# Layer 0's modulation vectors: four of six chunks moved out of the FFN's up-projection, two into the norms ahead of layer 0's mixer, two into its attention

## The chip, the cores and the metric

The kernel runs on one core of a Trainium2 chip. The metric is the device time of one execution in microseconds (us), lower is better. The kernel before takes 2705.91 us, the median of three runs (2704.4 to 2709.71).

## What is computed

One launch computes two blocks on 512 tokens of width 1024 in float32. The first block is a mixer of three kinds (a linear recurrence, forgetting attention, an RWKV cell) with a gated FFN. The second has two layers; each normalises, modulates by vectors that come from a condition, mixes (window attention with rope and a sink, neighbourhood attention, a gated convolution) and ends in a mixture of experts. The part that the change moves is `adaln`, for six chunks of 1024 columns per layer:

```python
def adaln(cond, w_mod_l, b_mod_l, n_chunks):
    m = jax.nn.silu(cond) @ w_mod_l[:, :n_chunks * D_MODEL] + b_mod_l[:n_chunks * D_MODEL]
    return jnp.split(m, n_chunks, axis=-1)
...
    for l in range(DEPTH_2):
        last = l == DEPTH_2 - 1
        sh1, sc1, g1, sh2, sc2, g2 = [m[:, None, :] for m in adaln(c, w_mod[l], b_mod[l], N_MOD)]
        ctx_mod = adaln(c_ctx, w_mod[l], b_mod[l], 2 if last else N_MOD)
        h = modulate(x, sh1, sc1)
        u = h @ w_in_l
        ...
        x = layer_norm(DEEPNORM_ALPHA * x + g1 * o, ln1_g[l], ln1_b[l])
        h2 = modulate(x, sh2, sc2)
        x = layer_norm(DEEPNORM_ALPHA * x + g2 * ec_moe(h2, w_router[l], w_gate[l], w_up[l], w_down[l]),
                       ln2_g[l], ln2_b[l])
```

So chunks 0 and 1 (sh1, sc1) are needed ahead of layer 0's mixer, chunks 2 to 5 only behind its attention.

## The kernel before, in words

The kernel is written in a tile framework: the program is written in one order, and the framework's scheduler sets a fixed order of instructions for each engine, with semaphores between them. Each engine then works through its own queue in order. The engines are TensorE (PE: products and transposes), VectorE (DVE), ScalarE (ACT, which also issues some DMAs), GpSimd (POOL) and SyncE (SP, which issues most DMAs, weight loads among them).

Precision comes from splitting: a weight tile `wr` is loaded, ScalarE rounds it to `wh` (L287), VectorE makes the rest `wl` (L288), and each product is three matmuls, hi by hi, lo by hi, hi by lo (L149, through `mm`).

`modulations(jobs, tile_, tag)` (L1013) makes one chunk of 1024 modulation columns for both conditions (token and context). For each of eight row blocks k it loads 128 x 1024 of w_mod, 512 KB, on SP's queue (L1021) into a tile that the caller's `tile_` gives, and issues four matmuls of 2 x 256, one to each column group of the array (L152, through `mmt`). It yields after every four k, so that the caller can place the steps. Then ScalarE copies the four pieces out of PSUM (L1028), eight small transposes turn them into columns (L1031), and VectorE adds the bias into the table of modulation columns (L1032). A chunk is thus 8 loads, 32 matmuls, 4 copies, 8 transposes and 1 add; in the trace a matmul of this kind is two records.

Stages around the change, in time:
- the FFN's up-projection of the first block, about 420 to 703 us: 44 blocks of 128 columns, each a weight load, a GEMM over 514 columns and a small convolution in ScalarE and VectorE. In its loop 12 modulation steps (6 chunks of layer 0) are spread;
- the FFN's down-projection with other modulation work, and the first block's last norms;
- `layer(0)`: layer norms (lnc), `modulated`, which normalises, transposes (xn, L1227) and splits tokens and context into `hh` and `hl`; then gated halves b = 0 and 1, each two GEMMs from `gemm2` (w_in loads L1259), a gate `sg` (a tanh) and the product `hx` (L1291, L1294); then 62 convolution taps on VectorE (`cy`, L1300 and L1303), placed by `tick` among the attention's work;
- attention: `stack_k` and `stack_q` make keys and queries by `gemm2`. With rope (`rope`, L1312) the queries are copied (L1315), their halves are swapped by eight DMAs on SP (L1318, L1319), multiplied on POOL and VectorE (L1320 to L1322) and split into `qst` (L1362, L1363). `scores`, `softmax` and `attend` follow for the head pairs i = 0 to 3 and four query blocks j. The sinks `nsk` (L1381, L1382) and tables `tb` (L1386) are loaded on ScalarE's queue. In the last head pair, i == 3, each query block also takes one modulation step of layer 1's chunks 0 and 1, with weight staging tiles (tags wr, wh, wl, two buffers each) as loads' targets (`any_w`).

In the changed kernel the lines from L1243 on have numbers higher by 3.

Of the kernel before, what the change touches and what calls it, by code (L numbers as in the profile page):

```python
# [9 lines left out]
F32 = mybir.dt.float32  # L10
# [129 lines left out]
def body(tc, A, out):  # L140
# [13 lines left out]
    offs, _, offs2, _ = host_constants()  # L154
# [17 lines left out]
    def nm(s):  # L172
        _n[0] += 1
        return "%s_%d" % (s, _n[0])
# [876 lines left out]
    def finish_modulations(after, after2):  # L1051
# [9 lines left out]
        for i in range(8):  # L1061
# [2 lines left out]
        DV.tensor_tensor(mc3, pt.rearrange("p (i g z) -> p g i z", i=8, g=4)[:, :, :, 0],  # L1064
                         v2[:, 80:112].rearrange("p (g i) -> p g i", g=4), ALU.add)
    sums_ = []
    mods = modulations([(0, six) for six in range(6)],
                       lambda: mrp.tile([128, 1024], F32, name=nm("wm"), tag="wm", bufs=8))
    for i in range(22):
        res = []  # L1070
        for hf in range(2):
            for _ in range(12 * (2 * i + hf + 1) // 44 - 12 * (2 * i + hf) // 44):
                next(mods, None)
            blk = 22 * hf + i
            W = load_w(wup, 5632, 128 * blk, 128)
            ps = gemm_fm(gps(), W, 0, 128, h2h, h2l, 0, 514)
            t = cv.tile([128, 512], F32, name=nm("cv"), tag="cv%d" % hf)
            AC.activation(t, ps[:, 2:514], AF.Copy, scale=fcol[:, 2, blk:blk + 1])  # L1078
            DV.scalar_tensor_tensor(t, ps[:, 1:513], fcol[:, 1, blk:blk + 1], t, ALU.mult, ALU.add)
            DV.scalar_tensor_tensor(t, ps[:, 0:512], fcol[:, 0, blk:blk + 1], t, ALU.mult, ALU.add)  # L1080
            res.append(t)
        AC.activation(res[0], res[0], AF.Gelu_apprx_tanh)
        DV.tensor_tensor(res[1], res[0], res[1], ALU.mult)
        AC.activation(aH[:, i, :], res[1], AF.Copy)
        DV.tensor_tensor(aL[:, i, :], res[1], f(aH[:, i, :]), ALU.subtract)
# [45 lines left out]
    mods = late_modulations()  # L1131
# [56 lines left out]
    def layer(l):  # L1188
        full = l == 0
# [47 lines left out]
        if full:  # L1237
            modulated(cxn, NC_, 512, 1)
            modulated(layer_norms(X, lnc), 512, 0, 0)
            cxs.close()  # L1240
        else:
            cb = [tp.tile([128, D], F32, name=nm("cb")) for j in range(2)]
            modulated(ready["x"], 512, 0, 0)  # L1243
            skewed([ready["ctx"](j, tp, cb[j]) for j in range(2)])
            modulated(cb, NC_, 512, 1)
            ready["close"]()
            cts.close()
# [232 lines left out]
        def any_w():  # L1480
            wtags.append(wtags.pop(0))
            return WPw.tile([128, 1024], F32, name=nm("wm"), tag=wtags[0], bufs=WB[0])
        mods = modulations([(1, 0), (1, 1)], any_w, "m") if full else iter(())

        def mod_steps(n):
            for _ in range(n):
# [21 lines left out]
        for i in range(4):  # L1508
# [4 lines left out]
            for j in range(4):  # L1513
                a0, a1 = max(0, j - 1), min(3, j + 1)
                w = 128 * (a1 - a0 + 1)
                ts = []
                for h in range(2):
                    ps = gps()
                    if j < 3:
                        c0, segs = 512 - w, [(512 - w, 128 * a0, w), (512, 512, 256)]  # L1520
                    else:
                        c0, segs = 256, [(256, 512, 256), (512, 128 * a0, w)]
                    scores(ps, q, k, h, 128 * j, segs)
                    b0 = (384, 256, 256, 0)[j]
                    ts.append(softmax([(ps[:, c0:c0 + w + 256], C2("wb")[:, b0:b0 + w + 256])], i + 4 * h))
                xb = list(range(a0, a1 + 1))
                attend(ts, xb + [4, 5] if j < 3 else [4, 5] + xb, (0, 64), oT[:, i, 128 * j:128 * j + 128])
                tick(NT)
                if i == 3:
                    mod_steps(1)  # L1530
            if full:
                ctx_pair(q, k, (i, i + 4), (0, 64), i, 1)
# [773 lines left out]
```

## Time and profile before

| | |
|---|---|
| runs, median (range) | 2705.91 us (2704.4 to 2709.71) |
| profiled execution, its own time | 2706.21 us |
| its span in the profile | 2704.4 us |
| mean granted TensorE clock | 0.964 of full |
| PE, DVE, ACT, POOL busy | 93%, 45%, 32%, 6% of the span |
| the FFN's up-projection | about 420 to 703 us |
| last norms and first GEMM of layer 0 | 841 to 873 us |
| attention of layer 0 | about 950 to 1140 us |

Busy PE means that a matmul is in its pipeline; matmuls overlap, so starts tell the pace better than durations. The chain of work that ended last is followed back from the last instruction; what does not lie on it costs nothing by itself.

### The profile page before, as it was taken

How to read it: one execution, taken by the hardware profiler on the slowest of the kernel's cores; microseconds unless marked ns; L12 is line 12 of the kernel's file. 1: busy time of each engine (PE TensorE's matmuls, PEld its weight loads, DVE VectorE, ACT ScalarE, POOL GpSimd, SP SyncE). 2: the span in 40 equal slices, each digit the busy share in tenths (PEclk: the TensorE clock that was granted, in tenths of full speed). 3: DMA queues.
4: the chain of work that ended last, by engine and by line, in shares of the span. 5: the costliest groups of instructions: out<-in, count | busy, mean ns of one | idle time of the engine just before them, and what ended most of it. 6: DMA issues, size and time to landing. Idle time of an engine off the chain costs nothing.

```text
span 2704.4 us, 52343 instructions
## 1 busy us (share of the span) xinstructions
PE 2507.4 (93%) x22270; PEld 1724.3 (64%) x22270; DVE 1210.7 (45%) x2278; ACT 875.9 (32%) x1585; POOL 167.4 (6%) x260
## 2 busy tenths in 40 slices
PE   7999999999998999996999999997999969999996
PEld 7877868999876977675555555544877744333332
DVE  4435655555655986556212121216977631112112
ACT  4335544343215266633100000006267421111102
POOL 0010100000001011002100000001111010000000
PEclk9989999999998999997999999998999969999998
DMA  4211144555672231433899999991331459999997
GB/s 138 63 41 37 45 164 156 180 164 180 201 257 75 74 73 33 134 106 140 311 407 375 381 367 382 364 379 45 100 78 35 162 193 404 406 409 409 409 409 278
DMA packets 266986, 579.02 MB, mean 214 GB/s; under 512 B 39920, under 2 KB 130416, under 8 KB 266496
## 3 DMA queue, kind: packets, MB, share of 16 engines
q1 hardware_dynamic: 255712, 550.82, 55.5%
q0 software_dynamic: 4928, 13.18, 2.0%
q10 hardware_dynamic: 6112, 11.68, 1.3%
q8 instruction: 175, 2.87, 0.4%
q14 instruction: 59, 0.48, 0.1%
HBM read 560.85 MB, written 5.24 MB: 209 GB/s over the span
## 4 chain that ended last, share of the span: by engine, by line
PE 52%; DVE 9%; ACT 3%; issue 2%; DMA 2%; POOL 1%; DVEq 0%; POOLq 0%; ACTq 0%; SPq 0%
PE g L149 18%; PE a L149 12%; PE g L152 12%; PE a L152 6%; DVE cy L1303 2%; PE a L1432 2%; POOL rv L235 1%; DMA gr<-rows,rowi 0%; DVE y L2055 0%; DMA wr<-in_w_out_dram 0%; DMA ew<-in_w_up_dram 0%; PE a L2266 0%; ACT pT L1393 0%; ACT ht L1229 0%; DVE wl L288 0%
## 5 line engine op out<-in xcount | busy, mean ns | idle before, releaser
L149 PE MATMUL g<-ew,xsel 128*64 128x512 f32 x1024 | 249.7, 599 | 0.2 <-DMA ew<-in_w_up_dram 0.2
L152 PE MATMUL g<-ew,xsel 128*32 128x256 f32 x4096 | 247.8, 380 | 0.2 <-ACT xsel L1816 0.2
L288 DVE TENSOR_TENSOR wl<-wr,wh 128x1024 fp32r<-128x1024 f32 x95 | 115.4, 1215 | 170.8 <-ACT wh L287 161.1
L152 PEld LDWEIGHTS g<-ew,xsel 128*32 128x32 f32 x4096 | 132.4, 110 | 92.7 <-issue 7.6
L149 PEld LDWEIGHTS g<-ew,xsel 128*64 128x64 f32 x1024 | 74.0, 137 | 136.2 <-issue 123.2
L287 ACT ACTIVATE wh<-wr 128x1024 fp32r<-128x1024 f32 x95 | 99.7, 1050 | 186.3 <-PE g L149 122.1
L235 POOL TENSOR_TENSOR rv<-ru,epsc 128x1 f32<-128x1 f32 (+3 forms) x63 | 53.6, 855 | 1712.4 <-DVE ru L233 1299.9
L149 PE MATMUL g<-h2h,wh 128*128 128x256 f32 x704 | 143.8, 285 | 0.0
L149 PE MATMUL g<-h2l,wh 128*128 128x256 f32 (+1 forms) x704 | 142.2, 284 | 0.0
L149 PE MATMUL g<-h2h,wl 128*128 128x256 f32 x704 | 141.9, 283 | 0.0
L152 PE MATMUL a<-ew,xsel 128*32 128x256 f32 x2048 | 133.7, 379 | 0.0
L2170 DVE TENSOR_TENSOR sg<-sg,g 128x512 f32<-128x512 f32 x16 | 11.0, 688 | 272.0 <-ACT sg L2169 272.0
L149 PE MATMUL g<-ew,hT 128*64 128x512 f32 x512 | 127.0, 596 | 6.2 <-DVE y L2055 5.9
L152 PE MATMUL g<-ew,hidT 128*32 128x512 f32 x1024 | 127.3, 592 | 0.5 <-DVE hidT L2171 0.5
L149 PEld LDWEIGHTS g<-h2h,wh 128*128 128x128 f32 x704 | 109.9, 191 | 5.5 <-ACT cv L1078 3.1
L2257 DVE TENSOR_TENSOR hid<-sg,g 128x512 f32<-128x512 f32 x16 | 11.0, 686 | 225.6 <-ACT sg L2256 225.6
L149 PEld LDWEIGHTS g<-h2h,wl 128*128 128x128 f32 x704 | 109.7, 191 | 0.0
L149 PEld LDWEIGHTS g<-h2l,wh 128*128 128x128 f32 x704 | 109.1, 190 | 0.0
L2169 ACT ACTIVATE sg<-g 128x512 f32<-128x512 f32 x16 | 9.6, 597 | 305.8 <-PE g L152 305.8
L1303 DVE SCALAR_TENSOR_TENSOR cy<-hx,cvc,cy 128x798 f32<-128x798 f32 (+1 forms) x120 | 107.0, 927 | 1.8
L1412 ACT ACTIVATE p<-p,mx 128x768 f32<-128x768 f32 (+4 forms) x120 | 91.5, 763 | 19.9 <-DVE mx L1405 15.8
L152 PEld LDWEIGHTS a<-ew,xsel 128*32 128x32 f32 x2048 | 67.0, 110 | 44.0
(655 smaller groups left out, 5368.9 us busy)
## 6 DMA issues: line engine op xcount, KB each, us to landing
ew<-in_w_gate_dram SPq DMA_DIRECT2D x256, 512.0 KB, 10.2
ew<-in_w_up_dram SPq DMA_DIRECT2D x256, 512.0 KB, 10.1
ew<-in_w_down_dram SPq DMA_DIRECT2D x256, 512.0 KB, 10.1
wm<-in_w_mod_dram SPq DMA_DIRECT2D x96, 512.0 KB, 4.9
wr<-in_ffn_up_dram SPq DMA_DIRECT2D x44, 512.0 KB, 4.1
wr<-in_w_in_dram SPq DMA_DIRECT2D x42, 512.0 KB, 4.1
wr<-in_ffn_down_dram SPq DMA_DIRECT2D x22, 512.0 KB, 4.7
wr<-in_w_out_dram SPq DMA_DIRECT2D x16, 512.0 KB, 3.5
```

Source lines behind the costliest of these rows:

```text
L149: return PE.matmul(o, l, r, start=start, stop=stop, skip_group_check=True)
L152: PE.matmul(o, l, r, start=start, stop=stop, skip_group_check=True, tile_position=(0, o.start_partition()))
L235: PL.tensor_tensor(v[:P], u[:P], epsc[:P, :w], ALU.pow)
L287: AC.activation(hi, raw, AF.Copy)
L288: DV.tensor_tensor(lo, raw, f(hi), ALU.subtract)
L1303: DV.scalar_tensor_tensor(cy[b], hx[b][:, i:i + N], cvw[l][:, 2 * i + b:2 * i + b + 1], cy[b], ALU.mult, ALU.add)
L1412: AC.activation(t[:, :e], t[:, :e], AF.Exp, scale=-1.0, bias=m, accum_out=sm)
L1432: PE.transpose(ps[:, 128 * i:128 * i + 128], t[:, 128 * i:128 * i + 128], ident)
L2169: AC.activation(sg[:, :w], ps[:, 0:w], AF.Silu)
L2170: DV.tensor_tensor(sg[:, :w], sg[:, :w], ps[:, w:2 * w], ALU.mult)
L2257: DV.tensor_tensor(hid[:, 512 * n:512 * n + 512], sg, psx[:, 512:1024], ALU.mult)
```

## The change

The FFN's loop keeps chunks 0 and 1 of layer 0 (4 steps). Chunks 2 and 4 are made in `layer(0)` right behind the second `modulated`, with their own pool `mw` of eight 512 KB tiles. Chunks 3 and 5 are put ahead of layer 1's chunks in the attention's list, whose steps are now taken in head pairs 2 and 3.

```diff
@@ -1064,12 +1064,12 @@
     sums_ = []
-    mods = modulations([(0, six) for six in range(6)],
+    mods = modulations([(0, six) for six in range(2)],
                        lambda: mrp.tile([128, 1024], F32, name=nm("wm"), tag="wm", bufs=8))
     for i in range(22):
         res = []
         for hf in range(2):
-            for _ in range(12 * (2 * i + hf + 1) // 44 - 12 * (2 * i + hf) // 44):
+            for _ in range(4 * (2 * i + hf + 1) // 44 - 4 * (2 * i + hf) // 44):
                 next(mods, None)
@@ -1237,6 +1237,9 @@
             modulated(layer_norms(X, lnc), 512, 0, 0)
+            mw = e3.enter_context(tc.tile_pool(name="mw", bufs=1))
+            for _ in modulations([(0, 2), (0, 4)], lambda: mw.tile([128, 1024], F32, name=nm("wm"), tag="wm", bufs=8)):
+                pass
             cxs.close()
@@ -1480,7 +1483,7 @@
-        mods = modulations([(1, 0), (1, 1)], any_w, "m") if full else iter(())
+        mods = modulations([(0, 3), (0, 5), (1, 0), (1, 1)], any_w, "m") if full else iter(())
@@ -1526,7 +1529,7 @@
                 tick(NT)
-                if i == 3:
+                if i > 1:
                     mod_steps(1)
```

The scheduler makes of it another order on several engines. Three places are shown; the numbers behind names count buffers and differ between the two programs, and a row with x4 stands for four instructions.

TensorE, in the first GEMM of layer 0's gated half (g, from hh and hl), behind the last transposes of xn. Before:

```order
L149 MATMUL g_9095<-hl_8951,wh_9099 128x256
L1227 MATMUL a_9079<-con,xn_9008 128x128
L1227 MATMUL a_9079<-con,xn_9010 128x128
L1227 MATMUL a_9079<-con,xn_9012 128x128
L1227 MATMUL a_9079<-con,xn_9014 128x128
L149 MATMUL g_9095<-hh_8950,wl_9100 128x256
L149 MATMUL g_9095<-hh_8950,wh_9099 128x256
```

Now:

```order
L149 MATMUL g_8971<-hl_8695,wh_8975 128x256
L152 MATMUL a_8835<-wm_8836,scol 2x256 x4
L152 MATMUL a_8835<-wm_8842,scol 2x256 x4
L152 MATMUL a_8835<-wm_8848,scol 2x256 x4
L152 MATMUL a_8835<-wm_8854,scol 2x256 x4
L152 MATMUL a_8835<-wm_8860,scol 2x256 x4
L152 MATMUL a_8835<-wm_8866,scol 2x256 x4
L152 MATMUL a_8835<-wm_8872,scol 2x256 x4
L152 MATMUL a_8835<-wm_8878,scol 2x256 x4
L149 MATMUL g_8971<-hh_8694,wl_8976 128x256
L149 MATMUL g_8971<-hh_8694,wh_8975 128x256
```

Chunk 2's matmuls (wm, scol) stand as one block behind two more GEMM rows that follow those transposes. Chunk 4's eight groups stand further on, each alone behind five GEMM rows, and the small transposes in pairs, the last pair eight GEMM rows ahead of its end.

VectorE, where hx is made. Before, the sinks' row (nsk, L1382) stands ahead of the gate and the products, and a weight split between hx and the first tap:

```order
L1382 TENSOR_SCALAR nsk_9523<-nsk_9523 128x8
L288 TENSOR_TENSOR wl_9219<-wr_9216,wh_9218 128x1024
L1287 TENSOR_SCALAR sg_9205<-sg_9205 128x768
L1291 TENSOR_TENSOR hx_9208<-g_9096,sg_9205 128x512
L1294 TENSOR_TENSOR hx_9208<-g_9096,sg_9205 128x256
L288 TENSOR_TENSOR wl_9273<-wr_9270,wh_9272 128x1024
L1300 TENSOR_SCALAR cy_8939<-hx_9208,cvc_4906 128x798
```

Now:

```order
L1032 TENSOR_TENSOR mc_4904<-a_8953,v_4912 128x16
L1290 TENSOR_SCALAR sg_9081<-sg_9081 128x768
L1294 TENSOR_TENSOR hx_9084<-g_8972,sg_9081 128x512
L1297 TENSOR_TENSOR hx_9084<-g_8972,sg_9081 128x256
L1385 TENSOR_SCALAR nsk_9399<-nsk_9399 128x8
L1303 TENSOR_SCALAR cy_8683<-hx_9084,cvc_4906 128x798
```

The sinks' row now stands between hx and the first tap; on ScalarE the load that it waits for now stands behind the gate's tanh.

TensorE, ahead of the first scores of the last head pair (g, from kh and qst). Before, its rows are attends (pT, vx) of the head pair ahead and modulation groups; the last GEMM row of the queries stands some 50 rows further up:

```order
L1432 MATMUL a_11736<-con,p_11722 128x128 x2
L149 MATMUL a_11741<-pT_11734,vx_9337 64x128
L152 MATMUL a_11902<-wm_11921,scol 2x256 x3
L149 MATMUL a_11741<-pT_11739,vx_9337 64x128
L149 MATMUL a_11741<-pT_11734,vx_9338 64x128
L149 MATMUL a_11741<-pT_11739,vx_9338 64x128
L152 MATMUL a_11902<-wm_11988,scol 2x256 x4
L152 MATMUL a_11902<-wm_11994,scol 2x256 x4
L149 MATMUL g_11848<-kh_10550,qst_11805 128x256
L149 MATMUL g_11848<-kl_10551,qst_11805 128x256
```

Now:

```order
L149 MATMUL a_11737<-hh_8694,wl_11743 128x512
L149 MATMUL a_11738<-hh_8694,wl_11743 128x256
L1031 MATMUL a_11896<-con,wm_11891 128x2 x8
L152 MATMUL a_11906<-wm_11907,scol 2x256 x4
L152 MATMUL a_11906<-wm_11913,scol 2x256 x4
L152 MATMUL a_11906<-wm_11919,scol 2x256 x4
L152 MATMUL a_11906<-wm_11925,scol 2x256 x4
L152 MATMUL a_11906<-wm_11992,scol 2x256
L149 MATMUL g_11837<-kh_10426,qst_11794 128x256
L149 MATMUL g_11837<-kl_10427,qst_11794 128x256
```

The queries' GEMM (a, from hh, wh and wl) ends right ahead of eight transposes, four groups and one more matmul, and the scores follow.

## Rows read from the trace of the kernel before

**Rows 1.** The page: engines' busy time; DMA rate in 40 slices; the chain by engine

```profile
PE 2507.4 (93%) x22270; PEld 1724.3 (64%) x22270; DVE 1210.7 (45%) x2278; ACT 875.9 (32%) x1585; POOL 167.4 (6%) x260
...
GB/s 138 63 41 37 45 164 156 180 164 180 201 257 75 74 73 33 134 106 140 311 407 375 381 367 382 364 379 45 100 78 35 162 193 404 406 409 409 409 409 278
...
PE 52%; DVE 9%; ACT 3%; issue 2%; DMA 2%; POOL 1%; DVEq 0%; POOLq 0%; ACTq 0%; SPq 0%
```

**Rows 2.** Table by stage: window, its length, busy time of each engine, clock, DMA share, GB/s

```profile
430.00:703.00 273.00, 273.00 (x2478) 257.85 (x2478) 142.63 (x177) 107.40 (x154) 0.00 (x0) 1.00 0.51 165
845.00:858.00 13.00, 10.41 (x54) 7.69 (x53) 8.24 (x17) 12.89 (x21) 0.00 (x0) 0.65 0.23 66
858.00:873.00 15.00, 15.00 (x83) 12.81 (x81) 6.25 (x11) 5.94 (x10) 0.66 (x1) 1.00 0.58 196
950.00:1000.00 50.00, 45.25 (x348) 36.57 (x347) 40.10 (x105) 32.45 (x69) 8.85 (x8) 1.00 0.31 71
1000.00:1050.00 50.00, 48.12 (x399) 38.37 (x398) 33.81 (x100) 35.38 (x89) 2.75 (x15) 1.00 0.05 14
1050.00:1100.00 50.00, 49.43 (x406) 40.81 (x405) 38.19 (x111) 37.25 (x97) 8.06 (x23) 1.00 0.19 55
1100.00:1140.00 40.00, 35.91 (x326) 22.08 (x320) 19.96 (x59) 23.08 (x60) 3.57 (x13) 0.96 0.47 161
```

**Rows 3.** The chain, 857 to 874 us: start us, us, what

```profile
858.35 14.83 PE g L149 x79
```

**Rows 4.** TensorE's timeline in the FFN: start us, us, engine, line, what

```profile
438.58 0.40 PE L149 MATMUL g<-h2h,wl 128*128 128x256 f32 x2
438.91 1.91 PE L152 MATMUL a<-wm,scol 128*2 128x256 f32 x32
440.75 0.50 PE L149 MATMUL g<-h2h,wh 128*128 128x256 f32 x2
...
483.20 0.65 PE L1031 MATMUL a<-con,wm 2*128 2x2 f32 x8
```

**Rows 5.** Timeline of layer 0's norms: VectorE, SP's queue and TensorE

```profile
842.47 0.15 DVE L1160 TENSOR_TENSOR lnc<-ls,rv 128x1 f32<-128x1 f32 x1
...
844.49 0.37 SPq L1259 DMA_DIRECT2D wr<-in_w_in_dram  x1
...
857.75 0.60 PE L1227 MATMUL a<-con,xn 128*128 128x128 f32 x4
```

**Rows 6.** TensorE's timeline in attention: a modulation group among others, a pair of transposes

```profile
1098.39 0.61 PE L152 MATMUL a<-wm,scol 128*2 128x256 f32 x6
1098.93 0.39 PE L149 MATMUL g<-kh,qst 128*128 128x256 f32 x1
...
1118.17 0.28 PE L1031 MATMUL a<-con,wm 2*128 2x2 f32 x2
```

**Rows 7.** Timeline before the first taps: ScalarE and its queue, VectorE

```profile
864.50 0.35 ACTq L1381 DMA_DIRECT2D nsk<-in_a_sink_dram  x1
...
868.33 0.79 ACT L1286 ACTIVATE sg<-g 128x768 f32<-128x768 f32 x1
...
869.14 0.17 DVE L1382 TENSOR_SCALAR nsk<-nsk 128x8 f32<-128x8 f32 x1 [4.66 <-DMA nsk<-in_a_sink_dram]
...
873.20 0.69 DVE L1291 TENSOR_TENSOR hx<-g,sg 128x512 f32<-128x512 f32 x1 [2.23 <-PE g L149]
```

**Rows 8.** Timeline before the last head pair's scores: ScalarE, SP, VectorE, TensorE

```profile
1094.98 0.60 ACT L1315 ACTIVATE q<-a 128x512 f32<-128x512 f32 x1
...
1100.51 0.59 SPq L1319 DMA_DIRECT2D qs<-q  x1
...
1106.76 0.42 DVE L1475 TENSOR_TENSOR hl<-oC,hh 128x256 fp32r<-128x256 f32 x1 [3.38 <-ACT hh L1474]
...
1110.06 0.58 PE L149 MATMUL g<-kh,qst 128*128 128x256 f32 x1 [3.12 <-DVE qst L1363]
```

**Rows 9.** The page, DMA issues: KB each, median us to landing

```profile
wr<-in_w_in_dram SPq DMA_DIRECT2D x42, 512.0 KB, 4.1
```

## The prediction

> **What bounds the kernel now.** I read the page's busy shares and its chain first, then a table by stage, then single rows. TensorE is busy 93% of the span and has 52% of the chain; VectorE comes next with 9%, DMA has 2% [rows 1]. So a stage matters by whether TensorE is full in it. In the stage that loses work, the FFN's up-products, it is full: 273.00 of 273 us at full clock, with DMA at 0.51 [rows 2]. The stage that gains two chunks has two parts. Up to 858 us TensorE has holes (10.41 of 13 us, clock 0.65), because ScalarE, busy 12.89 of 13, makes the normed and transposed tiles. From 858 to 873 TensorE is busy 15.00 of 15 [rows 2], and the chain runs through it alone, in one piece of 14.83 us [rows 3], until the first gated tile hx can be made at 873.20 [rows 7]; behind hx come the convolution taps on VectorE. In attention TensorE is busy 45.25, 48.12 and 49.43 of 50 us and 35.91 of 40 [rows 2]: 11.3 us of holes in 190, the largest I use 3.12 us before the scores of the last head pair [rows 8].
>
> A measurement of this kernel can tell about 0.2%, some 5.4 us, from no change.
>
> **FFN, four chunks out: −17.8 us.** A step of modulation is 32 matmul records (a program matmul of these leaves two) and takes 1.91 us among the GEMM's matmuls. The GEMM starts its last pair before it at 438.58, would go on 0.24 us later (two at 0.12), and goes on at 440.75: 1.93 us lost [rows 4]. The step's row ends at 440.82, so neighbours overlap by 0.07; the eight transposes of a chunk, 0.65 us, cost 0.58 then [rows 4]. A chunk is two steps and one set of transposes: 2 × 1.93 + 0.58 = 4.44 us, four of them 17.8, ±0.3. Nothing covers this work and nothing appears behind it: VectorE is busy 142.63 and ScalarE 107.40 of the 273 us [rows 2]. The loads that go with it have no price, DMA being half idle there.
>
> **Layer 0's norms, two chunks in: +9.8 us.** In the order of instructions all of it stands ahead of the end of the first half's GEMM, hence ahead of hx. Chunk 2's 32 matmuls (64 records) are one block behind the last transposes of xn, which ran at 857.75 [rows 5], when TensorE was just full. The price is the FFN's, 2 × 1.91 = 3.8 us. Chunk 4's eight groups of four matmuls stand singly, one in five GEMM rows. Attention shows such a group: it puts off the next row by 0.54 us (1098.39 to 1098.93) [rows 6]; eight make 4.3. The transposes go in pairs of 0.28 us [rows 6], 0.21 with the overlap: eight pairs, 1.7. Together 9.8. The lower bound fills TensorE's 2.6 us of holes before 858: 7.2. The upper has a late load: TensorE's queue is in order, so the block of chunk 2 would hold the GEMM behind it. Its eight loads wait for the last layer-norm columns (842.62) and then go ahead of w_in's load of 844.49 [rows 5]. Nine loads of 0.52 MB at the 409 GB/s that the page shows at its fastest [rows 1] take 11.5 us, to 854.2, against a need at 858; at 300 GB/s it would be 858.4. I count no stall, 2 us at the upper end. ScalarE's eight copies out of PSUM lie beside TensorE after 858, where ScalarE is busy 5.94 of 15 us [rows 2], at no cost; uncovered they would be some 2 us, by the tanh's 0.79 for 768 columns [rows 7].
>
> **The sink columns: +2.1 us.** Before, ScalarE issued the nsk load at 864.50 and VectorE, idle 4.66 us for it, had it at 869.14, well before hx at 873.20: free [rows 7]. Now that issue stands behind the gate's tanh, which waits for the new wm pool's release by chunk 4's last transposes, and VectorE's nsk row stands between hx and the first tap. Behind those transposes eight wide GEMM matmuls follow; 79 matmuls, wide and narrow, took 14.83 us [rows 3], so a wide one about 0.24 and eight 1.9. With the GEMM's end at T: tanh T − 1.9 to T − 1.1, load issued then, landed 4.64 us later (869.14 − 864.50) at T + 3.5. hx was 0.69 us for its wide part [rows 7] and a narrow part of half the columns follows, so it ends at about T + 1.4, and VectorE idles 2.1 us ahead of the taps. Bounds: 0 (issue beside the tanh, faster landing) and 4.6. The Trainium skill, "DMA: Bandwidth & Descriptors", section on the anatomy of one DMA, gives a fixed cost of about 2.0 us for a transfer, fitted there on GpSimd's issuing path. By it the load would land at T + 0.9 and this term be 0, the sum 2.1 us lower. I go by the row, 4.64 us on ScalarE's queue.
>
> **Attention, two chunks in: +8.5 us.** Sixteen groups of four at 0.54 us and eight pairs of transposes at 0.21 [rows 6] are 10.3 us of TensorE. The stage has 11.3 us of holes [rows 2], but the order puts the groups among scores and transposes of heads 1 to 3, where 1000 to 1100 us has 2.5 us of holes in all, and 3.12 of the rest belong to the next term. I let 1.8 us be hidden. Bounds: 2.1 (8.2 us hidden, every hole but the 3.12) and 10.3.
>
> **Attention, the last queries: +5.8 us.** Before, the GEMM of q for the last head pair (48 matmuls) was filler among the scores of heads 1 and 2. Now the wm groups are, and that GEMM stands near the end of head 2, its last 22 rows unbroken. Behind it a chain is fixed: copy of q, eight swap DMAs on SP (the last issued at 1100.51 for 0.59), landing, two VectorE products, the split, scores: 1094.98 to 1110.06, 15.1 us, of which VectorE's 3.38 us of waiting in an unrelated row, up to 1106.76, may go [rows 8]. So 11.7 us stay. Before, attends and wm groups filled all but 3.12 us of the 15.1. Now the order has between that GEMM and those scores eight transposes (0.58) and four and a quarter wm groups (2.2): 2.8 us. 11.7 − 2.8 = 8.9 idle against 3.1: +5.8. Upper bound 15.1 − 2.8 − 3.1 = 9.2; lower 0, if VectorE and SP reach their rows sooner than that. A longer hole may also lower the granted clock behind it; it is 0.96 in that stage before [rows 2], and I add nothing.
> On SP's queue q's weights move from right behind k's swaps to behind 17 wm loads, each of which waits for TensorE to read a buffer. From the read that gates them to the GEMM I count about 9 us of TensorE rows, against 4.1 us of landing [rows 9] and the split: enough, unless the four wm loads ahead share the time (4 × 0.52 MB at 409 GB/s, 5 us more, a stall of 2 to 3 us).
>
> **Sum.** −17.8 + 9.8 + 2.1 + 8.5 + 5.8 = +8.4 us. The profiled execution took 2706.21 us, 0.3 over the median of 2705.91, so I predict 2706.2 + 8.4 = **2714.6 us**, 0.3% slower. With all lower bounds: −17.8 + 7.2 + 0 + 2.1 + 0 = −8.5 (2698); with all upper: −17.8 + 11.8 + 4.6 + 10.3 + 9.2 + 2.5 = +20.6 (2727).
>
> **Rivals.**
> - *Hidden in attention.* Attention is bound by chains between engines, its holes take the groups, and q's GEMM ends early enough to be covered as before. The attention terms are 2.1 and 0: −17.8 + 9.8 + 2.1 + 2.1 = −3.8, 2702; with the norms' holes used and nsk in time, 2698. For it: ScalarE and VectorE are each busy 32 to 40 of 50 us there [rows 2], enough to set the pace together. Against: TensorE's 48.12 and 49.43 of 50. It decides at 5.9 us: with the two attention terms together under that, not at 14.3, the change breaks even or wins.
> - *Break-even.* One of the two attention terms has half its size and the nsk wait is gone: about 2708, 2704 to 2711.
> - *Late weights.* The order on SP becomes a wait of TensorE, for chunk 2's block at 858 or for q's weights at the end of head 2. It decides when DMA moves under 300 GB/s in the first or the wm loads share the second; 2 to 3 us at each place and up to 4 us of a longer rope chain: +8.4 + 9, 2724.
>
> **Chances.** The forecast's own case 0.50 (2711.3 to 2718), late weights 0.13, break-even 0.12, hidden 0.20, and 0.05 for holes that I don't see, below 2698. Slower by over 0.2%, above 2711.3: 0.50 + 0.13 = 0.63. Within 0.2%: break-even and half of the hidden case, 0.22. Faster by over 0.2%, below 2700.5: the other half and the 0.05, 0.15. The range 2699 to 2725 leaves out the 0.05, some of the hidden half and the end of the late weights. The likeliest case alone is 2711 to 2718.
>
> **What would show it.** Right: in the FFN four steps in place of twelve, and what follows 17.8 us earlier; TensorE full from 858 to the end of the first half's GEMM, which takes some 10 us longer from there; a VectorE wait of about 2 us for nsk behind hx; a wait of TensorE of some 9 us for the last q stack. Wrong: an attention stage under 6 us longer in all, no longer wait at the last scores, or a TensorE wait for a wm load.

## The result, and the profile after the change

The changed kernel takes 2722.56 us, median of 12 runs (2713.07 to 2730.76), against 2705.13 (2693.48 to 2709.71, 12 runs) for the kernel before. The ratio is 1.0069, 95% interval 1.0057 to 1.0081: 0.7% slower, 18.7 us by the ratio and 17.4 by the medians. The forecast was 2714.6 with a range of 2699 to 2725: the side was right and the range held, but the loss came out at twice the size.

The profiled execution of the changed kernel took 2718.75 us, with a span of 2717.0 us. In the table the span is cut at instructions that both programs have; each number is the difference of two starts in the timelines.

| stretch | before | after | change | forecast |
|---|---|---|---|---|
| start to the FFN's first evacuation (cv, ScalarE) | 428.60 | 425.79 | −2.8 | 0 |
| FFN: first to last evacuation | 274.06 | 255.40 | −18.7 | −17.8 |
| to the last layer-norm column (lnc) | 139.81 | 140.82 | +1.0 | 0 |
| lnc to the first hx | 30.73 | 44.86 | +14.1 | +9.8 |
| first to second hx | 18.94 | 24.36 | +5.4 | +2.1 |
| to the first split of the queries of head pair 0 (qst) | 114.72 | 115.52 | +0.8 | 0 |
| to the last two splits of those of head pair 3 | 102.46 | 119.94 | +17.5 | +14.3 |
| to layer 1's first hx | 785.37 | 786.09 | +0.7 | 0 |
| to the end of the span | 809.7 | 804.2 | −5.5 | 0 |

The first and the last row hold the same instructions in both; their −2.8 and −5.5 are differences between two executions and not the change's (over the thirteen profiles of this case the last stretch takes 802.4 to 810.0 us). The other rows add up to +20.8, a little over the 17.4 to 18.7 of the many runs. The rows of the kernel before are those of one execution, and not a middling one: from the second hx to the first qst, where the matmuls are the same in all kernels, it has 114.7 us and the twelve others 115.2 to 116.9.

The table by stage of the changed kernel (window, length, busy time of PE, PEld, DVE, ACT, POOL, granted clock, DMA share, GB/s) answers to [rows 2]:

```profile
425.79:681.19 255.40, 255.40 (x2201) 250.24 (x2200) 142.87 (x173) 102.06 (x139) 0.00 (x0) 1.00 0.36 113
839.00:867.00 28.00, 28.00 (x226) 16.76 (x226) 6.33 (x11) 9.35 (x17) 0.00 (x0) 1.00 0.56 192
1006.00:1050.00 44.00, 43.47 (x352) 34.36 (x351) 27.47 (x88) 29.68 (x79) 2.66 (x15) 1.00 0.09 28
1050.00:1100.00 50.00, 47.70 (x442) 33.39 (x441) 33.10 (x92) 34.25 (x84) 7.39 (x21) 1.00 0.48 155
1100.00:1127.00 27.00, 19.98 (x156) 12.98 (x154) 11.83 (x33) 13.16 (x36) 2.88 (x7) 0.95 0.43 137
```

TensorE is still full in the shorter FFN. In the norms it is full too, for 28 us now. In attention it is nearly full up to 1100 us (idle for 0.5 of 44 us and 2.3 of 50) and idle for 7.0 of the 27 us ahead of the last queries' scores.

TensorE's timeline in layer 0's first gated GEMM, changed kernel (start us, us, engine, line, what):

```profile
838.15 0.28 PE L149 MATMUL g<-hh,wl 128*128 128x256 f32 x1
838.27 0.60 PE L1227 MATMUL a<-con,xn 128*128 128x128 f32 x4
838.62 0.37 PE L149 MATMUL g<-hh,wh 128*128 128x256 f32 x1
838.83 0.28 PE L149 MATMUL g<-hl,wh 128*128 128x256 f32 x1
839.04 3.64 PE L152 MATMUL a<-wm,scol 128*2 128x256 f32 x64
842.60 0.39 PE L149 MATMUL g<-hh,wl 128*128 128x256 f32 x1
...
847.86 0.28 PE L149 MATMUL g<-hh,wh 128*128 128x256 f32 x1
847.97 0.28 PE L149 MATMUL g<-hl,wh 128*128 128x256 f32 x1
848.18 0.61 PE L152 MATMUL a<-wm,scol 128*2 128x256 f32 x8
848.73 0.39 PE L149 MATMUL g<-hh,wl 128*128 128x256 f32 x1
848.95 0.40 PE L149 MATMUL g<-hl,wh 128*128 128x512 f32 x1
...
862.01 0.39 PE L149 MATMUL g<-hh,wl 128*128 128x512 f32 x1
862.24 0.40 PE L149 MATMUL g<-hh,wh 128*128 128x512 f32 x1
862.57 0.28 PE L1031 MATMUL a<-con,wm 2*128 2x2 f32 x2
862.78 0.50 PE L149 MATMUL g<-hl,wh 128*128 128x512 f32 x1
863.21 0.28 PE L1031 MATMUL a<-con,wm 2*128 2x2 f32 x2
```

A narrow row's successor starts 0.12 us later (847.86 to 847.97), a wide one's 0.23 (862.01 to 862.24). Chunk 2's block takes 842.60 − 838.83 − 0.12 = 3.65 us out of the GEMM, no load is waited for, and the forecast was 3.8. A single group takes 848.73 − 847.97 − 0.12 = 0.64, and the narrow row behind it holds its successor back 0.22 us where 0.12 is the pace: 0.74 in all, against 0.54 forecast. A pair of transposes comes every 0.64 us with one wide row between (862.57 to 863.21): 0.41 each, against 0.21. So 3.65 + 8 × 0.74 + 8 × 0.41 = 12.9 us, and from the row behind the last xn transposes to the GEMM's end the two traces differ by 13.15 (28.05 against 14.90). This repeats: from the last xn transpose to hx it is 15.13 us in all eight kernels of this case without chunks there and 28.26 to 28.57 in all five with them. The other 1.0 us of the 14.1 lies ahead of it, from lnc to the last xn transpose (16.58 against 15.60), and goes with a low granted clock: 0.63 in the mean of 833 to 839 us, where the kernel before had 0.90 (853 to 858).

The Trainium skill, "TensorEngine Tiling (Array Packing)", section "Key Properties", says that changing the tiling mode drains the TensorE. The rows agree, and give the price that it leaves out: some 0.10 us at each end of a group or a pair. The four transposes of xn, which use the whole array, have no such ends in the same GEMM: from 838.15 to 838.83 it is 0.68 us, two narrow rows at 0.12 and four transposes at 0.11. That the ends are a drain and not another cost of the switch no run here shows. The prediction had the group from its own start to the next row's start and so left both out. The kernel before shows one of them ahead of the very group of [rows 6], which starts 0.32 us after the narrow row in front of it (1098.39 − 1098.07), 0.20 more than the pace:

```profile
1098.07 0.39 PE L149 MATMUL a<-hh,wl 128*128 128x256 f32 x1
```

The timelines of ScalarE, SP, VectorE, GpSimd and TensorE behind that GEMM, changed kernel (the number in brackets is idle time, with what ended it):

```profile
864.84 0.34 SPq L1254 DMA_DIRECT2D con<-in_con_dram  x1
...
864.86 0.81 ACT L1289 ACTIVATE sg<-g 128x768 f32<-128x768 f32 x1 [1.47 <-issue]
864.87 0.34 ACTq L1384 DMA_DIRECT2D nsk<-in_a_sink_dram  x1
...
866.87 0.69 DVE L1294 TENSOR_TENSOR hx<-g,sg 128x512 f32<-128x512 f32 x1 [0.60 <-PE g L149]
867.48 0.42 DVE L1297 TENSOR_TENSOR hx<-g,sg 128x256 f32<-128x256 f32 x1
871.67 0.17 DVE L1385 TENSOR_SCALAR nsk<-nsk 128x8 f32<-128x8 f32 x1 [3.78 <-DMA nsk<-in_a_sink_dram]
...
873.08 5.32 POOL L1391 TENSOR_TENSOR tb<-tb,con 128x896 f32<-128x896 f32 x2 [50.28 <-DMA tb<-in_nat_tab_dram]
...
873.50 10.10 DVE L1306 SCALAR_TENSOR_TENSOR cy<-hx,cvc,cy 128x798 f32<-128x798 f32 x6
...
892.30 0.69 PE L149 MATMUL g<-wh,hh 128*128 128x384 f32 x1 [5.09 <-DVE hx L1297]
```

The wait that was free in [rows 7] now stands on the chain: 3.78 us, where 2.1 were forecast. The load was issued as forecast, at 864.87, 1.8 us ahead of the GEMM's end at 866.7, but it landed 6.8 us later and not 4.64. SP issues a load of 1056 KB (con) just ahead of it, at 864.84, which lands after 6.6 us. The kernel before has the same two loads just as close, but in the other order, with nsk's first, at 864.50 [rows 7]:

```profile
864.56 0.34 SPq L1251 DMA_DIRECT2D con<-in_con_dram  x1
```

There nsk's landed after 4.5 us. The other profiles agree. With nsk's load issued ahead of con's it took 4.5 to 5.6 us in layer 0 of eight kernels, and 5.0 to 5.9 in layer 1 of eleven. Issued behind con's it took 6.7 to 6.8, in layer 0 of three. With no other load near it, in layer 1 of the two kernels that load the sinks early, it took 2.5. No run changes that order alone, so that it is the cause is likely, but not shown.

And six taps take 10.10 us, where the kernel before has

```profile
878.01 6.49 DVE L1303 SCALAR_TENSOR_TENSOR cy<-hx,cvc,cy 128x798 f32<-128x798 f32 x6
```

They run beside GpSimd's table sums (873.08 to 878.40); before, those stood beside the gate's products and one tap, at a cost of 2.0 us (a tap of 2.50 for 0.70, a split of 1.42 for 1.22). That makes 3.6 − 2.0 = 1.6 us more, and 3.78 + 1.6 is the 5.4 of the table. The Trainium skill, "SBUF — State Buffer", section "SBUF: two separate sides", has VectorE and GpSimd share one pair of ports as an exclusive lock. The rows agree: the first two of the six taps take 2.92 and 2.80 us and the other four 1.05 each, and the sums beside them take 2.49 and 2.88, where the same kernel has a sum at 982.80 us, beside no tap, in 2.09.

Ahead of the last queries' scores, changed kernel, TensorE and SP's queue, answering to [rows 8]:

```profile
1115.71 0.51 PE L149 MATMUL a<-hh,wl 128*128 128x512 f32 x2
1116.79 0.65 PE L1031 MATMUL a<-con,wm 2*128 2x2 f32 x8 [0.57 <-ACT q L1318]
1117.71 1.48 PE L152 MATMUL a<-wm,scol 128*2 128x256 f32 x24 [0.26 <-DVE mc L1032]
1119.83 0.61 PE L152 MATMUL a<-wm,scol 128*2 128x256 f32 x8 [0.65 <-DMA wm<-in_w_mod_dram]
1125.59 1.01 PE L152 MATMUL a<-wm,scol 128*2 128x256 f32 x2 [5.15 <-DMA wm<-in_w_mod_dram]
1127.43 0.58 PE L149 MATMUL g<-kh,qst 128*128 128x256 f32 x1 [0.83 <-DVE qst L1366]
...
1121.12 0.59 SPq L1322 DMA_DIRECT2D qs<-q  x1
1121.80 2.54 SPq L1021 DMA_DIRECT2D wm<-in_w_mod_dram  x5
```

From the end of the queries' GEMM to the scores there are 7.5 us of idle time (0.57 + 0.26 + 0.65 + 5.15 + 0.83), against 3.12 before and 8.9 forecast. The 5.15 us are a wait for a modulation load that SP issues only behind the eight swaps, a wait that the forecast did not have and that the prediction named as a sign of being wrong; it decided nothing by itself, since the queries were ready 1.8 us after it ended.

### The profile page after: what moved, and what is told of

Its sections match the earlier page's. It is cut to its first block, busy times and chain, and to the rows that moved or that the text cites. A ratio compares the mean times of both kernels' runs of the same rounds, so it can differ in the third digit from the quotient of the medians.

```text
span 2717.0 us, 52357 instructions
## 1 busy us (share of the span) xinstructions
PE 2511.8 (92%) x22270; PEld 1722.2 (63%) x22270; DVE 1214.4 (45%) x2278; ACT 877.2 (32%) x1585; POOL 167.4 (6%) x260
## 4 chain that ended last, share of the span: by engine, by line
PE 52%; DVE 9%; ACT 3%; DMA 2%; issue 2%; POOL 1%; SPq 0%; DVEq 0%; POOLq 0%; ACTq 0%; another core or an unknown queue 0%
PE g L149 18%; PE a L149 12%; PE g L152 12%; PE a L152 7%; DVE cy L1306 2%; PE a L1435 2%; DMA ew<-in_w_up_dram 1%; POOL rv L235 0%; DVE p L1408 0%; ACT pT L1396 0%; DMA ln_g<-in_ln_g_dram 0%; DVE y L2058 0%; PE a L2269 0%; ACT p L1415 0%; DVE wl L288 0%
## 5 line engine op out<-in xcount | busy, mean ns | idle before, releaser
L288 DVE TENSOR_TENSOR wl<-wr,wh 128x1024 fp32r<-128x1024 f32 x95 | 115.2, 1213 | 171.3 <-ACT wh L287 165.9
```

The costliest lines, as they stand in the source:

```text
L288: DV.tensor_tensor(lo, raw, f(hi), ALU.subtract)
```

## Experiments

The runs were made on several chips, so each kernel is compared with the kernel before that ran beside it on the same chip, and kernels of different chips by their ratios. In the code, ... stands for lines left out.

### The removal alone

Chunks 2 to 5 are made nowhere.

```diff
+    PL.memset(MC[0][:, 32:96], 1.0)
...
-    mods = modulations([(0, six) for six in range(6)],
+    mods = modulations([(0, six) for six in range(2)],
...
-            for _ in range(12 * (2 * i + hf + 1) // 44 - 12 * (2 * i + hf) // 44):
+            for _ in range(4 * (2 * i + hf + 1) // 44 - 4 * (2 * i + hf) // 44):
```

> Chunks 2 to 5 of layer 0 are made nowhere: a memset of 1.0 fills their modulation columns; the rest is the kernel before with four steps in the FFN's loop. It prices the removal alone. Theory (the FFN's up-projection is bound by TensorE): 17.8 us by the rows, 20.5 by the changed kernel's own arrival at the last layer-norm columns, so 2685 to 2688 against 2705. Rival (something else sets the FFN's pace when the steps are gone, or the gain is given back by the first block's last norms): a gain under 12 us.

Measured: 2684.78 against 2704.08, ratio 0.9923 (0.9910 to 0.9937), 19.3 us by the medians. First to last evacuation in the FFN is 255.39 us, as in the changed kernel (255.40). So the gain was there, at the size forecast, and what followed took it back twice.

### Each half alone

Chunks 2 and 4 into the norms only:

```diff
-    mods = modulations([(0, six) for six in range(6)],
+    mods = modulations([(0, six) for six in (0, 1, 3, 5)],
...
-            for _ in range(12 * (2 * i + hf + 1) // 44 - 12 * (2 * i + hf) // 44):
+            for _ in range(8 * (2 * i + hf + 1) // 44 - 8 * (2 * i + hf) // 44):
...
+            mw = e3.enter_context(tc.tile_pool(name="mw", bufs=1))
+            for _ in modulations([(0, 2), (0, 4)], lambda: mw.tile([128, 1024], F32, name=nm("wm"), tag="wm", bufs=8)):
+                pass
```

> Only chunks 2 and 4 move, into the norms; 0, 1, 3 and 5 stay in the FFN and attention is as before. Theory (each stage pays for itself, TensorE full in both): -8.9 for the FFN, +13.2 for the matmuls and transposes in the first gated half's GEMM, +3.8 for VectorE's wait for the sink columns and +1.6 for taps that run beside GpSimd's table sums: +9.7, about 2715. Rival 1 (attention carries the loss, the norms hide theirs): 2696 to 2700. Rival 2 (the lost time in the norms is absorbed by waits in attention): 2705.

Measured: 2717.30 against 2704.08, ratio 1.0049 (1.0035 to 1.0063), +13.2 us. Both rivals fall. By the rows the FFN gives 9.3 us back (264.75 against 274.06), lnc to hx is 44.04 and first to second hx 24.43 us, with the same nsk wait (3.84): −9.3 + 13.3 + 5.5 = +9.5, which is the lower end of the interval. The other 4 us of the median I could not place; the profiled execution, 2712.40, was the fastest of its five.

Chunks 3 and 5 into attention only:

```diff
-    mods = modulations([(0, six) for six in range(6)],
+    mods = modulations([(0, six) for six in (0, 1, 2, 4)],
...
-            for _ in range(12 * (2 * i + hf + 1) // 44 - 12 * (2 * i + hf) // 44):
+            for _ in range(8 * (2 * i + hf + 1) // 44 - 8 * (2 * i + hf) // 44):
...
-        mods = modulations([(1, 0), (1, 1)], any_w, "m") if full else iter(())
+        mods = modulations([(0, 3), (0, 5), (1, 0), (1, 1)], any_w, "m") if full else iter(())
...
-                if i == 3:
+                if i > 1:
```

> Only chunks 3 and 5 move, into attention; 0, 1, 2 and 4 stay in the FFN and the norms are as before. Theory: -8.9 for the FFN, +17.5 up to the last queries' scores (12.7 of TensorE work, 4.3 of waits), -3.5 in the last head pair, whose fill comes earlier, +3.5 behind it: +8 to +9, about 2714. Rival (attention's holes take the groups): 2696 to 2700.

Measured: 2712.84 against 2704.08, ratio 1.0035 (1.0022 to 1.0047), +8.8 us. The rival falls. First to last qst is 120.02 us, as in the changed kernel (119.94). Each half loses by itself: 13.2 + 8.8 = 22.0 against 17.4 to 18.7 for both, alike within the intervals.

### The sink columns out of the way

In the changed kernel, the sinks are loaded and negated from a tile of the pool that opens ahead of the norms.

```diff
         up_ = e2.enter_context(tc.tile_pool(name="u2", bufs=1))
+        nsk = up_.tile([128, 8], F32, name=nm("nsk"))
+        AC.dma_start(nsk, bass.AP(tensor=A["a_sink_2"].tensor, offset=A["a_sink_2"].offset + 8 * l, ap=[[0, 128], [1, 8]]))
+        DV.tensor_scalar(nsk, nsk, -1.0, None, ALU.mult)
...
-        sk = A["a_sink_2"]
-        nsk = at.tile([128, 8], F32, name=nm("nsk"))
-        AC.dma_start(nsk, bass.AP(tensor=sk.tensor, offset=sk.offset + 8 * l, ap=[[0, 128], [1, 8]]))
-        DV.tensor_scalar(nsk, nsk, -1.0, None, ALU.mult)
```

> The changed kernel, but the sink columns are loaded and negated from a tile of the pool that opens ahead of the norms, so nothing of it stands between hx and the first tap. Theory (VectorE's taps are the chain behind hx): the 3.8 us of wait go, 2722.6 to about 2719. Rival 1 (TensorE's GEMM of the second half bounds that stretch): no change, the wait of TensorE for the second hx (5.1 us) stays as it is. Rival 2 (the wait turns into more contention with GpSimd's table sums): a gain under 1.5 us.

Measured: 2716.03 against 2704.08, ratio 1.0040 (1.0026 to 1.0054), where the change has 1.0069 (1.0057 to 1.0081): the intervals do not meet. VectorE's timeline:

```profile
872.00 0.69 DVE L1297 TENSOR_TENSOR hx<-g,sg 128x512 f32<-128x512 f32 x1 [0.61 <-PE g L149]
872.60 0.41 DVE L1300 TENSOR_TENSOR hx<-g,sg 128x256 f32<-128x256 f32 x1
873.13 0.70 DVE L1306 TENSOR_SCALAR cy<-hx,cvc 128x798 f32<-128x798 f32 x1
...
874.87 9.96 DVE L1309 SCALAR_TENSOR_TENSOR cy<-hx,cvc,cy 128x798 f32<-128x798 f32 x6
...
892.48 0.69 DVE L1297 TENSOR_TENSOR hx<-g,sg 128x512 f32<-128x512 f32 x1
```

The first tap follows hx without a wait, and first to second hx is 20.48 us in place of 24.36, 3.9 less, as expected. The contention stays: six taps still take 9.96 us. The ratios say 7.8 us less, more than those rows give, within what two intervals of some ±3.5 us leave open. Both rivals fall.

### The queries one head pair earlier

Through head pair 2 the modulation chunks hold, one after the other, accumulators of the PSUM tag m, and the queries' GEMM takes both of that tag's. In the changed kernel the queries of head pair 3 are written behind them; here they are written ahead of head pair 2, and so for each.

```diff
+        qs_ = [stack_q(0, True, 256)]
         for i in range(4):
-            q = stack_q(64 * i, True, 256)
+            if i < 3:
+                qs_.append(stack_q(64 * i + 64, True, 256))
+            q = qs_[i]
```

> The changed kernel with each head pair's queries made one head pair earlier: the queries of i + 1 are written ahead of head pair i. Their GEMM needs both accumulators of PSUM tag m, which the modulation chunks 3 and 5 hold one after the other through head pair 2; written earlier, it comes before them. Theory (two parts in attention: some 12.7 us more TensorE work, 4.3 us more waiting at the last scores): only the waiting goes, 120 us from the first to the last qst become 115 to 116, the whole about 2718. Rival (the queries' late GEMM is the whole loss, and the groups would be hidden once it is out of the way): 104 to 108 us there, the whole about 2708.

Measured: 2717.44 against 2707.25, ratio 1.0038 (1.0024 to 1.0052). The time is the theory's, but the stretch that I had named for it is no measure here, since the last queries now come a head pair earlier by the edit itself. From head pair 0's first qst to layer 1's first hx it is 900.40 us, against 906.03 in the changed kernel and 887.83 before: 5.6 us less, and 12.6 remain. The rival falls.

With both mends:

> The changed kernel with both mends, queries one head pair earlier and the sink columns loaded ahead of the norms. Theory: the gains add, 2722.6 - 4.3 - 6 = about 2712, still over the kernel before by the 13 us of TensorE work in the norms and the 12.7 in attention less the 19.3 of the FFN. Rival (they were hiding one another): 2716 or more. If it comes out at 2700 or less, the move itself pays and only its order was bad.

Measured: 2710.31 against 2707.25, ratio 1.0018 (1.0007 to 1.0029). By the ratios about three quarters of the loss (0.69% to 0.18%) went with the two mends. By the rows it is about half: from the FFN's first evacuation to layer 1's first hx it is 1477.4 us, against 1487.0 in the changed kernel and 1466.1 before, one execution each. The move is still no gain.

### Queries earlier without the move, and with its attention half

These two tell whether the late queries belong to the move. The first is the kernel before with the edit of the last section; the second has chunks 3 and 5 in attention besides.

> The kernel before with nothing but each head pair's queries made one head pair earlier. Theory (the gain of the queries' order does not depend on where the modulation chunks are): 6 to 7 us faster, as between the last two runs, 2707 to 2700. Rival (it pays only where VectorE has the sums): no change.

> The run in which only chunks 3 and 5 move, into attention, with the queries one head pair earlier. Theory (two parts of the loss in attention: TensorE work of 10 us and more for two chunks in single groups, and the wait at the last scores; the order of the queries mends the wait alone): against the kernel before with the same order -9.4 for the FFN and +12 to +14 for the groups, so 3 to 4 us slower than that one. Rival (with the queries in time attention's holes take the groups): 5 us and more faster than that one.

Measured, beside the same runs of before (2703.34): 2701.56, ratio 0.9987 (0.9974 to 1.0001), and 2706.18, ratio 1.0009 (0.9995 to 1.0024). The first expectation missed: 1.8 us and not 6 to 7, though the rows of its profile are 4.4 us shorter from the first qst to layer 1's hx (883.46 against 887.83). The second held: 4.6 us slower than the first. By that stretch of the rows, the two chunks cost attention 897.25 − 883.46 = 13.8 us with the queries in time, and 903.46 − 887.83 = 15.6 us with them late. What these microseconds are, the rows from the first qst to the first product with a tile ew (a<-ew,hh, behind the attention's output) tell: all kernels have the same matmuls there, but for the 144 records of the two chunks. Window, length and busy time of each engine, in the changed kernel, the kernel before, and these two runs with and without the chunks:

```profile
1006.75:1215.82 209.07, 193.23 (x1447) 141.41 (x1447) 115.99 (x304) 123.93 (x285) 14.27 (x51) 0.96 0.39 125
1006.86:1198.47 191.61, 180.59 (x1303) 138.17 (x1302) 112.83 (x300) 119.58 (x277) 14.38 (x51) 0.96 0.30 92
998.05:1199.75 201.70, 193.22 (x1446) 142.11 (x1446) 116.35 (x304) 124.74 (x285) 14.54 (x51) 0.95 0.40 129
1012.44:1199.35 186.91, 180.24 (x1303) 136.84 (x1302) 114.84 (x302) 120.40 (x277) 14.04 (x51) 0.97 0.30 94
```

With the queries late the chunks cost 17.5 us, of which TensorE is busy for 12.6 and idle for 4.8. With the queries in time they cost 14.8, busy 13.0 and idle 1.8. So most of attention's loss is TensorE's own time for the chunks, and what goes with the late queries is 2 to 3 us of it.

The late queries are not the move's alone. With both mends the move is at 1.0018, the kernel before with the queries' mend at 0.9987: in that order the move costs 0.31%, some 8 us, and a part of what the mend gave, 1.8 us in the runs (with an interval that just reaches no gain) and 4.4 in the rows, seems to be had without the move. In the kernel before TensorE's granted clock is 0.66 at 1110 to 1115 us, behind its 3.12 us of waiting; with the queries in time it is 1.00 from 1060 to 1145.

### Sums on VectorE: a version that beats both

If TensorE bounds the FFN and VectorE has 130 us free there [rows 2], the chunks need not move: VectorE can sum them. Chunks 2 to 5 stay in the FFN's loop; only eight matmuls and the transposes of each remain on TensorE.

```diff
...
+            for k in range(8):
+                raw = mrp.tile([128, 1024], F32, name=nm("wm"), tag="wm", bufs=6)
+                SY.dma_start(raw, A["w_mod_2"][l][128 * k:128 * k + 128, 1024 * six:1024 * six + 1024])
+                for c in range(2):
+                    s_ = scol[:, 8 * c + k:8 * c + k + 1]
+                    if k == 0:
+                        DV.tensor_scalar(acc[c], raw, s_, None, ALU.mult)
+                    else:
+                        DV.scalar_tensor_tensor(acc[c], raw, s_, acc[c], ALU.mult, ALU.add)
+                yield
...
+            for g in range(4):
+                for c in range(2):
+                    mmt(ps[32 * g:32 * g + 2, :256], pick[:, 1 - c:3 - c], acc[c][:, 256 * g:256 * g + 256], c == 0, c == 1)
...
```

> From the kernel before, nothing moved out of the FFN: chunks 2 to 5 are summed on VectorE there (eight multiply-adds of 128 x 1024 for each condition and chunk, 1.28 us each by the rows of layer 1's sums), and TensorE only adds up the partitions, eight matmuls in place of 32 a chunk. Theory (the FFN is bound by TensorE and VectorE has 130 of 273 us free): TensorE loses 3.86 - 1.0 = 2.8 us a chunk, 11 in all, 2704 to about 2693. Rival (VectorE, at 142.6 + 82 of 273 us and in bursts, holds the blocks' evacuation back): no gain, or slower than before.

Measured: 2702.47 against 2707.25, ratio 0.9984 (0.9975 to 0.9994): faster, by less than half of what was expected. From ScalarE’s first cv<-cv in the FFN (the first evacuation has another place in this order) to its last evacuation it is 264.75 us, against 271.22 before: 6.5 us. TensorE's timeline has the reason: the transposes of a chunk come in pairs again, between GEMM rows.

```profile
476.26 0.40 PE L149 MATMUL g<-h2l,wh 128*128 128x256 f32 x2
476.60 0.29 PE L1094 MATMUL a<-con,wm 2*128 2x2 f32 x2
476.81 0.51 PE L149 MATMUL g<-h2h,wl 128*128 128x256 f32 x2
477.25 0.28 PE L1094 MATMUL a<-con,wm 2*128 2x2 f32 x2
477.46 0.51 PE L149 MATMUL g<-h2h,wh 128*128 128x256 f32 x2
```

Two narrow rows and a pair take 0.65 us (476.81 to 477.46), 0.41 more than the two rows' pace of 0.24. All sixteen pairs cost 0.41 to 0.42, the price of the norms' GEMM in another stage. The next kernel has the same work with two more blocks of the FFN between the sums and the transposes, and tiles of their own for the sums' loads:

```diff
-                raw = mrp.tile([128, 1024], F32, name=nm("wm"), tag="wm", bufs=6)
+                raw = mrp.tile([128, 1024], F32, name=nm("wm"), tag="wv", bufs=3)
...
+            yield
+            yield
             ps = aps()
             for i in range(8):
                 PE.transpose(ps[:, 2 * i:2 * i + 2], mr[:, 128 * i:128 * i + 128], ident[:2, :2])
...
```

> The sums on VectorE again, with the same work in another order: between the partition sums and the eight transposes of a chunk stand two more blocks of the FFN, so that the transposes come as one block and not in pairs, and the loads for the sums have tiles of their own, so that TensorE's own chunks come in steps of 16. Theory (each change of TensorE between GEMM rows and another kind of row costs at both ends: a pair of transposes takes 0.41 us out of the GEMM, eight in a block 0.58): 4 x (4 x 0.41 - 0.58) = 4.2 us less than the run with pairs, so 2698 against 2707. Rival (a pair costs its own 0.21 us, as the prediction had it): 4 x 0.26 = 1.0 us less, not to be told from the run with pairs.

Measured: 2697.12 against 2706.57, ratio 0.9965 (0.9954 to 0.9977); one of its 12 runs took 7690.67 us, which the comparison leaves out and whose cause is open. The stretch is 260.25 us, 4.5 less than with pairs, so the rival falls: the price of a pair is what it does to both of its neighbours. A block of eight among the GEMM's rows:

```profile
485.61 0.40 PE L149 MATMUL g<-h2h,wl 128*128 128x256 f32 x2
485.94 0.66 PE L1096 MATMUL a<-con,wm 2*128 2x2 f32 x8
486.52 0.51 PE L149 MATMUL g<-h2h,wh 128*128 128x256 f32 x2
486.87 0.40 PE L149 MATMUL g<-h2l,wh 128*128 128x256 f32 x2
```

Four narrow rows and the block take 1.26 us (485.61 to 486.87), 0.78 more than the four rows' pace of 0.48. The expectation took 0.58 for the block, without what it does to its neighbours, and 0.41 for a pair with it; counted alike, four blocks in place of sixteen pairs give 16 × 0.41 − 4 × 0.78 = 3.4 us and not 4.2. (Two edits were made together. The loads' own tiles have a part in the rest: with the shared tiles four groups of TensorE's own chunks stand singly, at 0.74 to 0.75 us each, 3.0 in all, where a step in one block costs 2.04; with tiles of their own only one group stands so.)


With the queries one head pair earlier besides:

> The same with each head pair's queries made one head pair earlier in attention. Layer 1's chunks are then the only filler there. Theory (in the kernel before, TensorE waits 3.1 us at the last scores, and its attention is otherwise TensorE's own work): up to 3 us less than without it, 2695. Rival (the queries' GEMM is filler that heads 1 and 2 need, and taken earlier it leaves holes there): no change or slower by 2 to 4 us.

Measured: 2690.54 against 2706.57, ratio 0.9937 (0.9919 to 0.9956): 0.6% faster than the kernel before, and the fastest here that makes all six chunks. It is 6.6 us under the kernel without the queries' edit, more than the 3 expected and more than that edit gave the kernel before (1.8, its interval reaching to 7); the intervals of the two gains overlap. In the rows from the first qst to the first product with a tile ew the edit gives 8.5 us here (193.84 to 185.35) and 4.7 there (191.61 to 186.91), and 2.2 of that lie between the two kernels without it, which have the same matmuls there. Whether it pays more here stays open.

## Why the prediction was right, and where it was short

- **FFN, −17.8:** right in kind, and 0.9 short: the removal alone is 19.3 us (the interval gives 17 to 24), by the rows 18.7. What is missing is the end behind each piece, as in the norms: counted to the second row behind it, a step that stands alone in the kernel before costs 2.04 us and not 1.93, and a block of eight transposes 0.78 and not 0.58.
- **Norms, +9.8:** the place and the mechanism were right (a full TensorE, everything ahead of hx, no load late), the size was short by 3.3 us. The step that failed is the price of single groups and pairs, "puts off the next row by 0.54 us" and "0.21 with the overlap". Start of a group to start of the next row leaves out what the row ahead loses and what the row behind passes on, 0.2 us a time. Eight groups and eight pairs with it: 9.8 + 16 × 0.2 = 13.0, and the rows say 13.15. The run with transposes in a block tested the price apart.
- **Sink columns, +2.1:** right in kind, 3.8 us in the rows. The term that was mis-sized is the landing, taken as 4.64 us from a row in which this load is issued just ahead of SP's load of 1056 KB; now it is issued just behind that, and took 6.8. By the 2.0 us that the Trainium skill, "DMA: Bandwidth & Descriptors", has as the fixed cost in its section on the anatomy of one DMA, fitted there on GpSimd's issuing path, the wait would have been nothing. The load by itself took 2.5, near that figure; beside the large load the measurement decides, and it is 6.8. The table sums of GpSimd, which slide onto the taps with the late start, cost 1.6 more and were not in the sum.
- **Attention, +8.5 and +5.8:** the total of 14.3 was 17.5 in the rows. The step that failed is the price of TensorE's own work, 10.3 less 1.8 hidden: TensorE is busy for 12.6 us more, and 13.0 more with the queries in time. The ends of the pieces belong to it, as in the norms, but the sum can't be made from single prices here: in the changed kernel's attention the groups stand partly split and partly together, and the transposes in blocks of eight and not in pairs. How the 4.1 us divide between the ends and a hiding that did not happen stays open. The wait for the last queries was right in kind and a little smaller than forecast: 4.3 us more idle time at that place and 4.8 in the whole stretch, against 5.8; with the queries in time 1.8 remain. That nothing was added for the clock was right: over the 5 us behind the hole the mean granted clock is 0.64 (1127.43 to 1132.43 us), and it was 0.66 before (1110.06 to 1115.06).
- **The rivals:** hidden in attention falls by the run with chunks 3 and 5 alone, which loses. Late weights fall for chunk 2 (no wait at 839.04) and for the queries (SP issued them at 1091.93, their GEMM began at 1103.38 without a wait); a late load did show, 5.15 us at 1125.59, at a place where the queries were not ready either, so it cost nothing by itself, though the prediction had such a wait among its signs of being wrong. The time itself, 2722.56, is where that rival put it (2724); only the rows tell it from the cause. Break-even falls by the time.
- **The range** held by luck. The forecast's own case, 2711.3 to 2718, missed; the upper end of the range had late loads and a longer chain in it, and the real excess came from elsewhere: the ends of the groups and pairs, the sinks' load behind another one, and the table sums beside the taps.

## What to carry to other kernels

Work that is taken out of a stage and put into another costs what the other stage's bounding engine charges: here both had TensorE full, so nothing was to be had, and a free engine in the old place (VectorE in the FFN) was worth more than a new place. Price a small piece among rows of another kind from the start of the row ahead of it to the second row behind it, less the pace, and keep such pieces together. When code is put ahead of a stage, look at what its queues issued early before, a small load above all: it may come to stand on the chain, and behind another queue's large load.

## What the runs showed of the hardware that I had not expected

- Four column-tiled matmuls among GEMM rows cost 0.74 us, 0.2 of it at the two ends; two transposes of 2 rows cost 0.41 and eight in a block 0.78. In a block of 32 such matmuls the two ends count once (3.65 us for 64 records up to the next row, 3.76 with the end behind it). Whole-array transposes among the same rows have no such ends.
- A load of 4 KB on ScalarE's queue took 2.5 us from issue to landing by itself, 4.5 to 5.9 when a 1056 KB load was issued on SP's queue some 0.05 us behind it, and 6.7 to 6.8 when that load was issued some 0.04 us ahead of it.
- Six taps on VectorE took 10.10 us beside 5.32 us of GpSimd's sums, and 6.49 without; GpSimd's two sums took 2.49 and 2.88 us there, and one beside no tap 2.09.
- Two executions of the same instructions differ by 3 to 6 us in stretches that no edit touches (2.8 before the FFN, 5.5 behind layer 1's hx, and 7.6 between the extremes of the thirteen profiles there), so changes of a few us were read from the starts of instructions, and only their sum from the runs.
